# A planner that keeps its clocks from every instruction instead of from guesses

## The chip, the cores and the metric

The kernel runs on one core of one Trainium2 chip. The metric is the device time of one execution in microseconds (us). The core has five engines with instruction queues of their own: TensorE (PE in the profile; PEld is its weight load), VectorE (DVE), ScalarE (ACT), GpSimd (POOL) and SyncE (SP), which issues most of the DMAs here. Each engine works through its instructions in the order in which they were written; between engines, semaphores make an instruction wait for what it needs.

## The reference

One layer of a streaming encoder, on 2048 new frames of one stream (the prompt) and 64 frames of a running one (the sample), 1024 features:

```python
def mixer_layer(x, ln_g, w_in, lb, norm_g, w_out, attn_fn, s0):
    aq, ak, av, ag, hq, hf, hi, hg = jnp.split(rms_norm(x, ln_g) @ w_in, SPLITS, axis=-1)
    o_a = attn_fn(heads(aq), k, v).reshape(B, T, W_A) * jax.nn.silu(ag)
    o_b, S = hgrn2_branch(hq, hf, hi, hg, lb, norm_g, s0)
    y = x + jnp.concatenate([o_a, o_b], axis=-1) @ w_out
    return y, k, v, S
...
y_prompt = rms_norm(hp, ln_f_g)
```

The input projection is 1024 x 4096. Its columns feed two groups: group A, chunked attention (8 heads of 64; each chunk of 64 frames sees itself and the 8 chunks before it, plus a learned bias by relative distance, then a gate `silu(ag)`), and group B, a gated linear recurrence (HGRN2, 4 heads of 128, a norm per head, and a gate). The output projection is 1024 x 1024, then come the residual and a last RMSNorm. Outputs are the frames of prompt and sample, the newest K and V rows, and the states of the recurrence. All is float32.

## The kernel before, in words

**Precision.** TensorE takes a rounded float32 format here. To keep float32 accuracy, each factor is split into a high and a low part (`xh`, `xl` for the normalized and transposed x; `w[:, 0]`, `w[:, 1]` for a tile of weights), and a product is xh·w_hi + xl·w_hi + xh·w_lo. With 8 tiles along the 1024 features, one output tile is a group of 24 matmuls into one PSUM bank `acc` (`project`, recorded at L246, like nearly every matmul). There are two `acc` banks, and a group can only begin once the bank's former content has been read by ACT or DVE.

**Stages.** The frames are worked through in four super-blocks (512, 512 + 64 sample, 512, 512 frames). For each, `JOBS` lists 32 projection tiles of 128 columns, in the order hf, hq, hi, hg (group B), pg, pq, pk, pv (group A), for each of the four heads or pairs of heads. Blocks are 512 frames wide, 256 + 320 in the second super-block; the first two tiles and the last two of each super-block are worked in two halves, because the rows of the next x replace those of the old one half by half. In the first super-block the weights come raw from memory and are split by DVE and POOL (`w_split`, L461 to L469), then stored to be loaded in split form later.

**Beside the projections** run threads for:
- x (`x_tile`, `x_split`): load of 128 rows, square and sum (ACT L375), 1/root (ACT L343, L344), normalize (DVE L383), transposes on PE (L250) and the split into xh (ACT L408) and xl (DVE L412);
- the evacuations: silu of the gates (ACT L566 to L568), q (ACT L715, L721), k (ACT L738, L745, DVE L749), v (ACT L761);
- attention: score matmuls into the one `s` tile (two banks), softmax (DVE L819, L840, ACT L836), transposes of the probabilities, their split (ACT L848, DVE L851), the product with v (`pv`);
- the recurrence, with small matmuls of 32 rows (L254).

**The output phase.** W_out is applied by a seven-product scheme in the manner of Strassen, for eight pairs of 128-row tiles. A step (`out_step`) is 12 matmuls of 512 columns into one bank. Beside it, `out_parts` copies the next left factor's high part (ACT), `out_low` takes its low part (DVE L1597 or POOL L1589), sums of the factor's blocks are made (DVE L1610, POOL L1615), `out_adds` adds a bank to the kept partial `u` (DVE L1711) and to the residual rows (`out_add`, DVE L1685; the adds of `u` on POOL L1690), and `out_norm` makes the last norm (DVE L1753 or L1762). The residual rows and their room carry the names of former tiles (`xn`, `bias`, `pr`, `rest`). Part of W_out is loaded into the room of attention's v (L1930), once that is done.

**The order** is written by a planner, `Plan`, when the program is built. Every thread is a Python generator that yields what it waits for: a point in time, an engine, a buffer's token (`Tok`), or a condition. The main thread yields between pairs of matmuls; at each yield `pump` runs every thread that is ready, by priority, and what a thread writes goes to the end of its engine's queue. Readiness goes by the plan's estimated clocks: `C.now` for PE, `C.free` for ACT, DVE, POOL and SP. The threads themselves move these clocks: `C.act(n, t)`, `C.dve`, `C.pool` and `C.dma` add a time from flat formulas, with a width n that the thread gives, and `C.mm` adds a matmul. A thread that wants an engine is ready when that engine's clock is at most QUEUE (800 ns) ahead. The estimates set only the order; the waits on the chip come from the data.

Of the kernel before, what the change touches and what calls it, by code (L numbers as in the profile page):

```python
# [32 lines left out]
QUEUE = 800.0  # L33
# [12 lines left out]
JOBS = [[(k, g) for g in range(4) for k in ("hf", "hq", "hi", "hg", "pg", "pq", "pk", "pv")] for _ in SUPER]  # L46
JOBS[-1][-12:] = [("hf", 3), ("hq", 3), ("pq", 2), ("pk", 2), ("pv", 2), ("hi", 3), ("hg", 3), ("pg", 2), ("pg", 3),
# [3 lines left out]
class Plan:  # L51
# [4 lines left out]

    def __init__(self):
        self.now = 0.0
        self.free = {"A": 0.0, "D": 0.0, "P": 0.0, "S": 0.0}
        self.threads = []  # L60
        self.count = 0

# [65 lines left out]
    def mm(self, n, slow=False):  # L128
        self.now += 10.0 + 1.66 * n if slow else 12.0 + n / 2.37
# [12 lines left out]
    def dve(self, n, t=0.0):  # L142
        return self._on("D", 150.0 + 1.05 * n, t)

    def pool(self, n, t=0.0):
        return self._on("P", 300.0 + 1.6 * n, t)
# [34 lines left out]
def hymba_step(  # L181
# [24 lines left out]
    act = nc.scalar  # L206
    dve = nc.vector
    pool = nc.gpsimd
    pe = nc.tensor
    sp = nc.sync  # L210

    act.preload_act_table_set("natural_log_exp_and_others")
# [7 lines left out]
    C = Plan()  # L220
    uid = [0]

    def T(pool_, shape, dt, tag, **kw):
        uid[0] += 1
        return pool_.tile(list(shape), dt, tag=tag, name=f"{tag}_{uid[0]}", **kw)
# [19 lines left out]
    def mm(out, w, x, n, slow=False, **kw):  # L245
        pe.matmul(out, w, x, **kw)  # L246
        C.mm(n, slow)

    def transpose(out, x, idn):
        pe.transpose(out, x, idn)  # L250
        C.now += 110.0

    def mm32(out, w, x):
        pe.matmul(out, w, x, start=True, stop=True)  # L254
        C.now += 30.0
# [102 lines left out]
    def x_tile(sb, half, c, here=None, gain=None):  # L358
# [10 lines left out]
        if half and not sb:  # L369
            yield lambda: x_there.get((0, 0, 0), (0, 0))[0] == 4  # L370
        yield "A", t
        yield from tk["ck"].get()
        junk = T(wk, [P, D], mybir.dt.bfloat16, "ck", bufs=1)
        ss = T(wk, [P, 1], F32, "ss", bufs=4)
        act.activation(junk[:rows], xn[:rows], AF.Square, accum_out=ss[:rows])  # L375
        r = rstd_of(ss, rows, D)
        tk["ck"].put()
# [5 lines left out]
        dve.scalar_tensor_tensor(xn[:rows], xn[:rows], r[:rows], g, ALU.mult, ALU.mult)  # L383
        t = C.dve(1070, t)
# [49 lines left out]
    def weights():  # L434


        for j, (sb, nt) in enumerate(order):
            if sb:
# [5 lines left out]
                w_at[j] = (w, t, t)  # L444
# [10 lines left out]
    def w_split(j, nt, raw, t, tok):  # L455
# [12 lines left out]
        for k in range(0, KT, 2):  # L468
            pool.tensor_sub(w[:, 1, k : k + 2], raw[:, k : k + 2], f32(w[:, 0, k : k + 2]))  # L469
            t = C.pool(320, t)  # L470
            if k == 0:
                w_at[j] = (w, th, t + 2500.0)
            if k < KT - 2:
                yield "P", t - 300.0
        if tok:
            tk[tok].put()
# [4 lines left out]
    def out_weights():  # L481


        for a in range(4):
# [12 lines left out]
            def split(i, src):  # L497
# [3 lines left out]
                for c in cols:  # L501
                    yield "A", t
                    act.copy(f32r(st[:, c]), src[:, c])  # L503
                    t = C.act(256, t)
                    yield "P", t
                    pool.tensor_sub(f32r(st[:, c.start + 512 : c.stop + 512]), src[:, c], st[:, c])  # L506
                    t = C.pool(320, t)
                sp.dma_start(wod[i][:, :, a], st.rearrange("p (h c) -> p h c", h=2))
                state["t"] = t
                state[state["n"] - 1] = C.dma(512, t) + 2000.0  # L510

            def minus(out, x, y):
                for c in cols:
                    yield "P", state["t"]
                    pool.tensor_sub(out[:, c], x[:, c], y[:, c])
                    state["t"] = C.pool(320, state["t"])
# [10 lines left out]
            for tag, n in (("raw", 2), ("xn", 2), ("ck", 1)):  # L527
                tk[tag].put(n, C.now + 4000.0)
            yield C.now + 6000.0

    def project(j, ranges, evac, close=True, ready=None):
        yield lambda: j in w_at
        w, th, tl = w_at[j]
# [3 lines left out]
        for off, bn in ranges:  # L537
# [50 lines left out]
    def split_k(src, kd, c0, n, t):  # L588
        c = slice(c0, c0 + n)
        for h in range(2):  # L590
# [5 lines left out]
            if h == 0:  # L596
                yield "A", t - 300.0
# [14 lines left out]
    def load_bias(sb, p, d):  # L612
# [19 lines left out]
        C.now += 870.0  # L632
# [4 lines left out]
        tk["g"].put(1, t + 800.0)  # L637
# [45 lines left out]
    def pair_jobs(sb, p):  # L683
# [26 lines left out]
        def ev_q(acc, off, bn, t):  # L710
# [12 lines left out]
            yield "D", t - 600.0  # L723
            for h in range(2):
# [3 lines left out]
                if h == 0:  # L728
                    yield "D", t - 300.0
# [4 lines left out]
        def ev_k(acc, off, bn, t):  # L734
# [12 lines left out]
            yield "D", t - 600.0  # L747
# [1321 lines left out]
```

## Time and profile before

| | |
|---|---|
| median of three runs | 1264.97 us (1262.31 to 1268.16) |
| the profiled execution's own time | 1265.17 us |
| its span, first to last instruction | 1263.5 us |
| PE busy | 1243.6 us, 98% |
| DVE, ACT, POOL busy | 885.0, 698.6, 405.9 us |
| mean granted clock of TensorE | 0.995 |

The page gives the busy time of each engine, the chain of work that ended last, and groups of instructions. A wait of an engine is put down to what ended it: "PE acc L246 <- ACT vT L761" is a matmul into an acc bank that began when ACT's instruction of line 761 had ended. Busy time of PE counts a matmul also where the clock granted to TensorE is half; the granted clock of a stretch stands beside it. In a timeline a row gives its start, its duration, the engine, the line, out<-in, the shape and in brackets the idle time before it with its releaser.

### The profile page before, as it was taken

To read this page: it belongs to the slowest core of one execution; us is meant where nothing else is said; L and a number is where in the kernel's file an instruction comes from. 1 tells how busy PE (TensorE), PEld (TensorE's weight loads), DVE (VectorE), ACT (ScalarE), POOL (GpSimd) and SP (SyncE) were. 2 spreads that over 40 slices of the span, in tenths; PEclk is the share of its full clock that TensorE was granted. 3 is DMA by queue.
4 is the path that set the end of the run, shared out by engine and by line. 5 is a ranking of instruction groups with operands and counts; after the bars stand their busy time and mean duration, and the time that the engine had idled before them with its cause. 6 is when DMAs were issued, how large, how long until landed. Compare 5 with 4: busy or idle time off the path is not lost.

```text
span 1263.5 us, 22305 instructions
## 1 busy us (share of the span) xinstructions
PE 1243.6 (98%) x8182; PEld 1094.1 (87%) x8182; DVE 885.0 (70%) x1836; ACT 698.6 (55%) x1544; POOL 405.9 (32%) x704
## 2 busy tenths in 40 slices
PE   9999999999999999999999999999999999999997
PEld 8888888999999999998888888898888888878786
DVE  6787969676757667687575757685757765867775
ACT  5353646555655557575465556574646545643443
POOL 6655555111110111100242331133152203474543
PEclk9999999999999999999999999999999999999999
DMA  7876788635454455534858586557676476887331
GB/s 300 285 290 234 255 276 316 226 136 189 145 195 165 146 194 178 173 133 151 307 185 303 184 294 211 203 197 260 222 250 219 155 255 241 309 276 219 127 132 67
DMA packets 94862, 271.72 MB, mean 215 GB/s; under 512 B 10337, under 2 KB 43105, under 8 KB 77090
## 3 DMA queue, kind: packets, MB, share of 16 engines
q1 hardware_dynamic: 94464, 270.30, 60.7%
q8 instruction: 64, 1.05, 0.3%
q14 instruction: 44, 0.36, 0.1%
q10 hardware_dynamic: 290, 0.01, 0.0%
HBM read 186.66 MB, written 83.62 MB: 214 GB/s over the span
## 4 chain that ended last, share of the span: by engine, by line
PE 88%; DVE 4%; POOL 2%; ACT 2%; issue 2%; DMA 0%; SPq 0%; POOLq 0%; DVEq 0%; ACTq 0%
PE acc L246 62%; PE tr L250 6%; PE pv L246 6%; PE s L246 6%; PE g L246 5%; PE g L250 1%; PE g L254 1%; DVE slot L1597 1%; PE g L1864 1%; POOL sig L1615 1%; DVE xn L1685 1%; POOL xn L1690 1%; DVE xl L412 0%; POOL bias L1690 0%; DVE xn L1753 0%
## 5 line engine op out<-in xcount | busy, mean ns | idle before, releaser
L246 PE MATMUL acc<-xh,w 128*128 128x512 f32 (+2 forms) x2752 | 569.7, 346 | 5.9 <-ACT vT L761 2.1
L246 PEld LDWEIGHTS acc<-xh,w 128*128 128x128 f32 x2752 | 439.0, 190 | 56.5 <-ACT vT L761 2.3
L246 PE MATMUL acc<-xl,w 128*128 128x512 f32 (+2 forms) x1376 | 297.5, 348 | 0.2 <-DVE xl L412 0.2
L246 PEld LDWEIGHTS acc<-xl,w 128*128 128x128 f32 x1376 | 222.0, 190 | 25.8 <-issue 1.0
L819 DVE CUSTOM_DVE_ANT_0 pr<-s,bias 128x640 f32<-128x640 f32 (+4 forms) x128 | 94.3, 737 | 64.2 <-PE s L246 63.5
L848 ACT CAST ph<-tr 128x512 fp32r<-128x512 f32 (+3 forms) x176 | 88.1, 508 | 68.0 <-PE tr L250 36.4
L469 POOL TENSOR_TENSOR w<-wraw,w 128x256 fp32r<-128x256 f32 x120 | 98.9, 853 | 66.2 <-DVE w L464 41.1
L851 DVE TENSOR_TENSOR ph<-tr,ph 128x512 fp32r<-128x512 f32 (+3 forms) x176 | 100.5, 589 | 22.2 <-ACT ph L848 21.2
L836 ACT ACTIVATE pr<-pr,nm 128x640 f32<-128x640 f32 (+4 forms) x132 | 100.6, 762 | 25.2 <-DVE nm L819 24.6
L246 PE MATMUL pv<-ph,v 128*128 128x256 f32 (+2 forms) x344 | 97.7, 370 | 0.0
L250 PE MATMUL tr<-ident,pr 128*128 128x128 f32 x580 | 88.9, 272 | 1.1 <-DVE ph L851 1.1
L506 POOL TENSOR_TENSOR xn<-wraw,xn 128x256 fp32r<-128x256 f32 x48 | 37.8, 791 | 162.3 <-ACT xn L503 162.2
L988 POOL TENSOR_TENSOR mixa<-mixa,sga 128x256 f32<-128x256 f32 (+1 forms) x36 | 29.8, 826 | 171.9 <-DVE mixa L890 161.8
L890 DVE TENSOR_TENSOR mixa<-mixa,pv 64x256 f32<-64x256 f32 (+1 forms) x144 | 56.8, 395 | 35.0 <-ACT mixa L886 31.4
L250 PEld LDWEIGHTS tr<-ident,pr 128*128 128x128 f32 x580 | 70.5, 140 | 11.6 <-issue 1.5
L840 DVE TENSOR_SCALAR pr<-pr,sm 128x640 f32<-128x640 f32 (+4 forms) x132 | 76.9, 583 | 4.7
L1435 POOL TENSOR_TENSOR k<-ob 128x512 f32<-128x512 f32 (+2 forms) x20 | 17.8, 892 | 183.8 <-ACT ob L1426 183.8
L566 ACT ACTIVATE sig<-acc 128x512 f32<-128x512 f32 (+2 forms) x63 | 31.9, 506 | 60.7 <-PE acc L246 60.5
L246 PEld LDWEIGHTS pv<-ph,v 128*128 128x128 f32 (+1 forms) x344 | 58.1, 189 | 6.6
L246 PE MATMUL s<-kd,q 128*128 128x320 f32 (+3 forms) x232 | 56.4, 313 | 0.7 <-DVE nm L819 0.7
L246 PE MATMUL s<-kd,ql 128*128 128x320 f32 (+3 forms) x232 | 55.6, 310 | 0.0
L1458 POOL TENSOR_TENSOR ob<-ob,gg 128x512 f32<-128x512 f32 (+2 forms) x20 | 23.5, 1174 | 85.7 <-DVE ob L1454 66.5
(328 smaller groups left out, 2144.1 us busy)
## 6 DMA issues: line engine op xcount, KB each, us to landing
w<-wd SPq DMA_DIRECT2D x96, 1024.0 KB, 4.9
wd<-w SPq DMA_DIRECT2D x32, 1024.0 KB, 6.3
wraw<-in_w_in_dram SPq DMA_DIRECT2D x30, 512.0 KB, 4.9
wod<-xn SPq DMA_DIRECT2D x28, 512.0 KB, 3.6
xn<-in_x_prompt_dram SPq DMA_DIRECT2D x23, 512.0 KB, 6.0
bias<-biasd SPq DMA_DIRECT2D x12, 640.0 KB, 8.2
carry<-kd SPq DMA_DIRECT2D x12, 512.0 KB, 7.2
carry<-v SPq DMA_DIRECT2D x12, 512.0 KB, 5.8
```

Of the source, the lines that this page charges most:

```text
L246: pe.matmul(out, w, x, **kw)
L250: pe.transpose(out, x, idn)
L469: pool.tensor_sub(w[:, 1, k : k + 2], raw[:, k : k + 2], f32(w[:, 0, k : k + 2]))
L506: pool.tensor_sub(f32r(st[:, c.start + 512 : c.stop + 512]), src[:, c], st[:, c])
L566: act.activation(sig[:, :bn], acc, AF.Exp, scale=-1.0)
L819: dve.tensor_tensor_reduce(s[:, :nk].rearrange("p (a c) -> p a c", a=ns), sps[:, :ns, :kn], d.bias[:, h, bcol : bcol + nk].rearrange("p (a ...
L836: act.activation(s[:, :nk], s[:, :nk], AF.Exp, bias=nm[:, 0:1], scale=-1.0, accum_out=sm)
L840: dve.tensor_scalar(s[:, :nk], s[:, :nk], sm, None, ALU.mult)
L848: act.copy(ph[:krows, 0, :wid], pt[:krows, :wid])
L851: dve.tensor_sub(ph[:krows, 1, :wid], pt[:krows, :wid], f32(ph[:krows, 0, :wid]))
L890: dve.tensor_add(mix[hs, :qn], mix[hs, :qn], pv[hs, i, :qn])
L988: pool.tensor_mul(mix[:, :n], mix[:, :n], d.sg[:, g0 : g0 + n])
```

## The change: clocks charged per instruction, engines picked by them

Every engine is wrapped (`Queue`). Each instruction that is written charges the plan: a duration by engine, operation, width and whether an operand lies in PSUM; and its start is the latest of the engine's clock and of the last accesses to the same parts of the tiles it touches (`seen`, by boxes), with a lag for the engine that made the access. The functions `act`, `dve`, `pool` and `dma` now only answer when the engine's last instruction ends plus the lag; the widths in the threads are no longer read.

```diff
-QUEUE = 800.0
+QUEUE = 600.0
...
+JOBS[0][:2] = [("hq", 0), ("hf", 0)]
...
+    LAG = {"": 0.0, "T": 200.0, "A": 250.0, "D": 250.0, "P": 250.0, "S": 100.0}
...
+    def charge(self, e, ns, outs, ins):
+        t = max([self._last(e, x, True) for x in outs] + [self._last(e, x, False) for x in ins] + [0.0])
+        if e == "T":
+            self.now = end = max(self.now, t) + ns
+        elif e == "S":
+            start = max(self.now, self.free[e], t)
+            self.free[e] = start + 420.0
+            self.links = max(start + 520.0, self.links) + ns
+            self.landed = end = self.links + 2000.0
+        else:
+            self.free[e] = end = max(self.free[e], t) + ns
+        for x in ins:
+            self._note(e, x, False, end)
+        for x in outs:
+            self._note(e, x, True, end)
+        return end
+
+    def pick(self, t, **cost):
+        return min(cost, key=lambda e: max(self.free[e], self.now, t) + cost[e])
...
     def pe(self):
-        return self.now + 400.0
-
-    def _on(self, e, ns, t):
-        start = max(self.now, self.free[e], t)
-        self.free[e] = start + ns
-        return start + ns + 150.0
-
-    def act(self, n, t=0.0):
-        return self._on("A", 150.0 + 0.87 * n, t)
...
-    def dma(self, kbytes, t=0.0):
-        start = max(self.now, self.free["S"], t)
-        self.free["S"] = start + kbytes * 2.8
-        return self.free["S"] + 3500.0
+        return self.now + self.LAG["T"]
+
+    def act(self, n=0, t=0.0):
+        return self.free["A"] + self.LAG["A"]
...
+    def dma(self, kbytes=0, t=0.0):
+        return self.landed + self.LAG["S"]
...
+        if self.e == "S":
+            return _bytes(aps) / 370.0
```

(`_bytes` is four times the elements, more where the rows are short: 512 KB count 1417 ns.)

The output phase asks the clocks for the engine. Until the last super-block's attention is done, the answer is POOL:

```diff
+    def out_engine(t):
+        if done_a.get(len(SUPER) - 1, 0) < NPAIR * WIN:
+            return "P"
+        return C.pick(t, D=670.0, P=1500.0)
+
     def out_low(i, k, m, src, t, tags):
-        e = "P" if i < 2 and k != 3 else "D"
+        e = out_engine(t)
...
-                if op == ALU.add:
-                    yield "D", t
+                if out_engine(C.now) == "D":
+                    yield "D", C.now
                     dve.tensor_tensor(out, x, y, op)
...
-        if e == "D":
+        if e == "D" or out_engine(t) == "D":
             yield "D", t
             dve.tensor_add(x, x, part)
```

Other edits go with it. The threads' own allowances go: tokens are given back at an engine's time instead of `now + 800`, waits of `t - 300` or `t - 600` become `t - 100`; `project` waits until a weight tile's low part has been written out instead of 2.5 us after its high part:

```diff
-                w_at[j] = (w, th, t + 2500.0)
+                w_at[j] = [w, th, None]
...
+        w_at[j][2] = t
...
                 if i == 2:
-                    yield tl
+                    yield lambda: w_at[j][2] is not None
+                    yield w_at[j][2]
```

At the start, the first two tiles' normalize is written in two halves, the sum tile is made before the wait for `ck`, the gain row is loaded on SP's queue instead of ACT's, and the two first jobs change places:

```diff
-        dve.scalar_tensor_tensor(xn[:rows], xn[:rows], r[:rows], g, ALU.mult, ALU.mult)
-        t = C.dve(1070, t)
+        for cs in (slice(0, 512), slice(512, D)) if not sb and not half else (slice(0, D),):
+            dve.scalar_tensor_tensor(xn[:rows, cs], xn[:rows, cs], r[:rows], g[:, cs], ALU.mult, ALU.mult)
+        t = C.free["D"] - 600.0 * (not sb and not half)
...
-        act.dma_start(g_in[0:1], ln_in_g.rearrange("(o d) -> o d", o=1))
+        sp.dma_start(g_in[0:1], ln_in_g.rearrange("(o d) -> o d", o=1))
```

In `out_weights` the copies of a block are written before its subtractions, and the store waits for POOL's time. In the last super-block, whose x has no successor, the last two tiles are no longer worked in halves:

```diff
-                if u in (1, len(JOBS[sb]) - 1):
+                first, end = u < 2, not last and u >= len(JOBS[sb]) - 2
+                if (first or end) and u % 2:
...
-                elif u not in (0, len(JOBS[sb]) - 2):
+                elif not (first or end):
                     yield from project(j, blocks, evac)
```

More of the change, by code (lines that the diff above doesn't have):

```diff
@@ L148, in dma, with name, _box @@
-    def dma(self, kbytes, t=0.0):
-        start = max(self.now, self.free["S"], t)
-        self.free["S"] = start + kbytes * 2.8
-        return self.free["S"] + 3500.0
+    def name(self, pool, tag, bufs, name):
+        n = self.rooms.setdefault((pool, tag), [0])
+        n[0] += 1
+        self.rooms[name] = (pool, tag, n[0] % bufs)
+    def _box(self, ap):
+        name = getattr(ap.tensor, "source_name", None)
+        room = self.rooms.get(name)
+        if room is None or room[1] in ("xh", "xl"):
+            return None, None
+        dims = [tuple(d) for d in ap.ap]
+        if room[0] == "dr":
+            return room, (0, 1, ap.offset, ap.offset + 1 + sum((n - 1) * st for st, n in dims))
+        p, f = divmod(ap.offset, dims[0][0])
+        return room, (p, p + dims[0][1], f, f + 1 + sum((n - 1) * st for st, n in dims[1:]))
@@ new lines, in _last, with _note @@
+    def _last(self, e, ap, write):
+        room, box = self._box(ap)
+        t = 0.0
+        for b, (w, r) in self.seen.get(room, {}).items():
+            if b[0] < box[1] and box[0] < b[1] and b[2] < box[3] and box[2] < b[3]:
+                for at, by in (w, r) if write else (w,):
+                    if by != e:
+                        t = max(t, at + self.LAG[by])
+        return t
+    def _note(self, e, ap, write, end):
+        room, box = self._box(ap)
+        if room is None:
+            return
+        boxes = self.seen.setdefault(room, {})
+        w, r = boxes.get(box, ((0.0, ""), (0.0, "")))
+        boxes[box] = ((end, e), r) if write else (w, max(r, (end, e)))
@@ new lines, in pick, with dve, pool, _free @@
+    def pick(self, t, **cost):
+        return min(cost, key=lambda e: max(self.free[e], self.now, t) + cost[e])
+    def pe(self):
+        return self.now + self.LAG["T"]
+    def act(self, n=0, t=0.0):
+        return self.free["A"] + self.LAG["A"]
+    def dve(self, n=0, t=0.0):
+        return self.free["D"] + self.LAG["D"]
+    def pool(self, n=0, t=0.0):
+        return self.free["P"] + self.LAG["P"]
+    def dma(self, kbytes=0, t=0.0):
+        return self.landed + self.LAG["S"]
+def _free(ap):
+    n = 1
+    for d in list(ap.ap)[1:]:
+        n *= d[1]
+    return n
@@ L154, with _bytes, _size @@
+def _bytes(aps):
+    n = min(_size(x) for x in aps)
+    run = min(list(x.ap)[-1][1] if list(x.ap)[-1][0] == 1 else 1 for x in aps)
+    return 4.0 * n * max(1.0, 128.0 / run)
+def _size(ap):
+    n = 1
+    for d in list(ap.ap):
+        n *= d[1]
+    return n
 class Tok:
@@ L767, in ev_v @@
             d.v_t = max(d.v_t, C.now + 1000.0)
-            if last and p == NPAIR - 1 and d.v_n == n:
-                have.add("projected")
+            closing()
             if d.v_n == n and not last:
@@ L799, in ev_g, with closing @@
             d.sg_n += bn
+            closing()
+        def closing():
+            if last and p == NPAIR - 1 and d.v_n == n and d.sg_n == n:
+                have.add("projected")
         return d, dict(g=ev_g, q=ev_q, k=ev_k, v=ev_v)
@@ L1140, in ev_f @@
             act.activation(f[:, :bn], acc, AF.Exp, scale=-1.0)
-            tk["acc"].put(1, C.now + 800.0)
+            tk["acc"].put(1, C.act())
             act.activation(f[:, :bn], f[:, :bn], AF.Ln, bias=one_t)
@@ L1448, in rec_block @@
         act.activation(rs[:, :bn], pn[:, :bn], AF.Ln, bias=eps_t, scale=1.0 / P)
-        tk["g"].put(1, C.now + 800.0)
+        tk["g"].put(1, C.act())
         act.activation(rs[:, :bn], rs[:, :bn], AF.Exp, scale=-0.5)
@@ L1921, in program @@
                 j += 1
+            if last:
+                x_left[sb, 0] = x_left[sb, 1] = True
         for i, k in steps:
```

157 lines of the change are left out of this document (109 added, 48 removed).

## The prediction

> **What bounds the kernel now.** I read the page's busy shares and its chain first, then the chain of waits of TensorE, then stage windows, then the timelines around each gap.
>
> ```profile
> span 1263.5 us, 22305 instructions
> PE 1243.6 (98%) x8182; PEld 1094.1 (87%) x8182; DVE 885.0 (70%) x1836; ACT 698.6 (55%) x1544; POOL 405.9 (32%) x704
> PE 88%; DVE 4%; POOL 2%; ACT 2%; issue 2%; DMA 0%; SPq 0%; POOLq 0%; DVEq 0%; ACTq 0%
> ```
>
> PE is busy 1243.6 of 1263.5 us. The change leaves the arithmetic alone, so it can only win from the 19.9 us in which PE idles, and from stretches in which PE runs at a lower clock. Two parts of the idle time are out of reach: the start and the tail. The columns of a stage window are us, PE, PEld, DVE, ACT, POOL busy, clock, DMA share, GB/s.
>
> ```profile
> 0.00:13.50 13.50, 11.74 (x58) 10.06 (x59) 4.40 (x6) 6.22 (x13) 6.63 (x21) 0.87 0.87 324
> 254.30:257.70 3.40, 3.40 (x16) 3.40 (x15) 3.33 (x13) 2.13 (x8) 0.66 (x3) 0.50 0.02 5
> 810.60:814.00 3.40, 3.40 (x16) 3.40 (x17) 2.34 (x5) 2.97 (x8) 0.00 (x0) 0.51 1.04 433
> 1066.60:1070.00 3.40, 3.06 (x25) 3.07 (x26) 2.49 (x6) 1.09 (x4) 0.00 (x0) 1.00 1.01 367
> 1128.00:1131.40 3.40, 3.40 (x16) 2.79 (x15) 3.40 (x3) 1.14 (x2) 3.40 (x3) 1.00 1.16 316
> 1137.60:1256.90 119.30, 118.25 (x517) 95.55 (x515) 84.44 (x128) 48.79 (x121) 57.45 (x66) 1.00 0.42 135
> 1256.90:1263.50 6.60, 0.01 (x1) 0.00 (x0) 3.43 (x5) 1.22 (x4) 0.00 (x0) 0.83 0.42 159
> ```
>
> The tail costs 6.59 us and the start 1.76; 11.5 us of idle remain. Two stretches of 3.4 us, one behind each of the two largest gaps of the middle, ran at a granted clock of 0.50 and 0.51: each loses 3.4 x 0.5 = 1.7 us of work. So the most the change can win is about 11.5 + 3.4 = 14.9 us and a little of the program's own length. The waits name the gaps:
>
> ```profile
> PE acc L246 <- ACT vT L761: 2.1, 1, 2.1
> PE acc L246 <- ACT xh L408: 1.7, 2, 1.3
> PE acc L246 <- DMA v<-wod: 1.7, 1, 1.7
> PE acc L246 <- ACT vT L738: 1.4, 1, 1.4
> PE tr L250 <- DVE ph L851: 1.1, 1, 1.1
> PE s L246 <- DVE nm L819: 0.7, 1, 0.7
> PE acc L246 <- DVE pr L1685: 0.6, 1, 0.6
> PE acc L246 <- DVE xn L1685: 0.6, 2, 0.4
> ```
>
> Each is a single event, a place where the written order put a matmul a little too early. Nothing is spread over the run.
>
> **The change part by part.** *Clocks from instructions, waits per tile (Plan.charge, QUEUE 600, LAG).* No instruction changes by this; the order does. I compared the two written orders at each gap.
>
> ```profile
> 253.89 0.61 PE L246 MATMUL acc<-xh,w 128*128 128x320 f32 x2 [1.34 <-ACT xh L408]
> 810.56 1.16 PE L246 MATMUL acc<-xh,w 128*128 128x256 f32 x4 [2.08 <-ACT vT L761]
> 810.13 0.37 ACT L761 COPY vT<-acc 128x256 f32<-128x256 f32 x1 [0.69 <-DVE kd L749]
> 1062.44 1.21 PE L246 MATMUL acc<-xh,w 128*128 128x256 f32 x8 [0.45 <-ACT vT L715]
> 1066.94 0.98 PE L246 MATMUL acc<-xh,w 128*128 128x256 f32 x6 [1.37 <-ACT vT L738]
> 1066.53 0.35 ACT L738 COPY vT<-acc 128x256 f32<-128x256 f32 x1
> 1126.96 0.50 PE L246 MATMUL acc<-v,slot 128*128 128x512 f32 x1 [1.66 <-DMA v<-wod]
> ```
>
> At 253.9 the first 320-wide matmul stands right behind the last transposes of the next x rows, so PE waits while ACT and DVE turn them into xh and xl. In the new order 12 matmuls of 256 columns stand between; by the pitch (1.21 - 0.98) / 2 = 0.115 us each that is 1.4 us, as long as the gap. Gain 1.34, and the slow stretch behind it. At 810.6 the acc bank was emptied late because its copy (L761) was queued on ACT behind k work that itself waited 0.69 us for DVE; the new order leaves at least 1.6 us of PE work between a bank's last matmul and its next first one there. Gain 2.08, and its slow stretch. The two stretches are worth 1.7 each at most and nothing at least, if another gap starts one; I take 1.5 each, because gaps as long remain at few places. At 561 the 0.7 us wait for the softmax has at least 1.3 us of work before it: gain 0.67. At 1106 the transpose's wait for a split (1.1) has more too: gain 1.1. At 1062 to 1067 two gaps, 0.45 + 1.37, stand against one place of the new order where a 512-wide acc group of pk follows directly on the evacuation of pq: an evacuation of a 256-wide bank takes 0.35 us, and one of 512 with its wake-up I put at 0.95 us (between 0.45 and 1.37, the gaps of such a place). Gain 0.87.
>
> At 1127 PE waits for W_out rows loaded into v's room, which comes free only with the last pv. The loads' queue does not change; but 58 matmuls stand between the last pv and the first use where there were 28, and at 118.25 / 517 = 0.229 us each that is 30 x 0.229 = 6.9 us more. Gain 1.66; at worst, if the loads queue behind others by 5 us more, still all of it.
>
> *Last super-block unsplit.* 96 matmuls of 256 columns become 48 of 512.
>
> ```profile
> 1135.69 5.70 PE L246 MATMUL acc<-w,slot 128*128 128x512 f32 x24 [0.25 <-DVE bias L1685]
> 1240.28 3.00 PE L246 MATMUL acc<-w,slot 128*128 128x512 f32 x12 [0.41 <-DVE xn L1685]
> 7.05 3.75 PE L1864 MATMUL g<-ident 128*128 128x128 f32 x22
> ```
>
> A 512-wide matmul costs (5.70 - 3.00) / 12 = 0.225, two of 256 cost 0.230: 48 x 0.005 = 0.2 us gained.
>
> *The start.* Swapped hf and hq cost nothing, since both tiles' weights are loaded before either is done. The gain row's load moves onto SP's queue ahead of the x loads and delays them by one small issue; ends 0 and +0.5, and I take 0, because PE spins until the first transposes anyway. One spin less (10 for 11, 3.75 / 11) is 0.3 gained, if the first half-width normalize is done by then.
>
> *The output phase.* In before, the sums for the Strassen products, the low parts and the adds of u are fixed to POOL or DVE; now each goes to the engine free first. By the orders 56 POOL instructions of 256 columns go away there, and about 28 DVE ones of 512 come.
>
> ```profile
> 1239.45 0.69 DVE L1685 TENSOR_TENSOR xn<-xn,acc 128x512 f32<-128x512 f32 x1 [1.27 <-POOL xn L1690]
> 1238.68 0.73 POOL L1690 TENSOR_TENSOR xn<-xn,asb 128x256 f32<-128x256 f32 x1
> 1236.98 1.74 POOL L1615 TENSOR_TENSOR sig<-sig,reset 128x256 f32<-128x256 f32 x1
> L1685 DVE TENSOR_TENSOR xn<-xn,acc 128x512 f32<-128x512 f32 x14 | 9.4, 684 | 9.0 <-PE acc L246 4.4 <-POOL xn L1690 3.2 <-ACT asb L1703 1.3
> L1597 DVE TENSOR_TENSOR slot<-sig,slot 128x512 fp32r<-128x512 f32 x11 | 8.1, 748 | 0.0
> L1610 DVE TENSOR_TENSOR vT<-vT,vT 128x512 f32<-128x512 f32 x3 | 3.1, 1036 | 0.2 <-POOL sig L1615 0.2
> L1753 DVE SCALAR_TENSOR_TENSOR xn<-xn,rstd,gin 128x1024 f32<-128x1024 f32 (+1 forms) x6 | 8.1, 1355 | 3.1 <-ACT rstd L1748 3.1
> 1127.13 3.43 DVE L1753 SCALAR_TENSOR_TENSOR xn<-xn,rstd,gin 128x1024 f32<-128x1024 f32 x2
> ```
>
> The gap of 0.41 at 1240 is DVE's add waiting 1.27 us, in order, behind POOL's u-add, itself behind a POOL sum of 1.74 us: with the u-adds on DVE this chain is gone. Of the waits on L1685 (0.6 + 0.6 + 0.3) I count 1.2 gained. What it costs: 28 x 0.684 = 19 us more on DVE, which is busy 84.4 of 119.3 us; 103 of 119 (87%) stays under the matmuls as long as no step of 12 matmuls (2.7 us) waits for its bank. I take 1 us lost there; ends 0 and 18 (the rival below). The Trainium skill, "Perfetto Trace Analysis", section "Optimizing Scalar/DVE Operations", says that a saturated DVE should give work away, and that moving work between DVE and GpSimd may not help, since they share an SBUF port. This case's trace agrees in part: the normalize took 3.43 / 2 = 1.72 us beside a POOL sum, against a mean of 1.355. By that rule the move would give nothing in this phase, and the sum would be 1.2 us worse.
>
> *What the tighter order costs.* The new lags (0.2 to 0.25 us) leave less room than the old guesses. Two kinds of places:
>
> ```profile
> L819 DVE CUSTOM_DVE_ANT_0 pr<-s,bias 128x640 f32<-128x640 f32 (+4 forms) x128 | 94.3, 737 | 64.2 <-PE s L246 63.5
> xn<-in_x_prompt_dram SPq DMA_DIRECT2D x23, 512.0 KB, 6.0
> 810.53 1.06 ACT L375 ACTIVATE ck<-xn 128x1024 bf16<-128x1024 f32 x1
> 247.00 0.29 ACT L343 ACTIVATE rstd<-ss,eps 128x1 f32<-128x1 f32 x1
> ```
>
> About ten groups of score matmuls now have 1.20 to 1.36 us of PE work since the scores bank was filled before, which must cover 0.737 for the softmax row and a wake-up on both sides. I put 0.15 us on each: 1.5, ends 0 and 3. And at the first boundary of super-blocks an x row tile is loaded 9.0 us of PE work before its transposes (14.3 before). The path needs 6.0 to land, 1.06 for the square, 0.29 for each of the root's two small steps and 1.355 for the normalize: 9.0. I take 0.5 us, ends 0 and 1.5 plus a slow stretch of 1.7.
>
> **Sum.** Gained: 1.34 + 2.08 + 2 x 1.5 + 0.67 + 1.1 + 0.87 + 1.66 + 0.2 + 0.3 + 1.2 = 12.4. Lost: 1.0 + 1.5 + 0.5 = 3.0. Net 9.4: span 1254.1. The profiled execution took 1265.17 us with a span of 1263.5, so 1.7 lies around it, and it stands 0.2 above the median of 1264.97. So 1255.6.
>
> **The rivals.** *Eaten by tight lags.* The gaps go, but the micro-waits come at their upper ends (3 for scores, 3.2 for x rows) and new gaps of a microsecond arise where the per-tile clocks are wrong, each starting a slow stretch as at 254 and 810. For it: a gap of 1.34 was enough for that, and PE has no slack elsewhere. Against it: behind the gaps of 1.37 at 1066 and 1.66 at 1126 the windows show a clock of 1.00. With 4 to 5 us more it ends near 1260 to 1264, within 0.5%.
>
> The Trainium skill, "TensorE: Matmul & The Clock Gate", Part 1, ties the slowdown to an idle window of about 3.4 us; here the trace shows gaps of 1.34 and 2.08 us in front of it, so the length of a gap alone does not tell.
>
> *DVE becomes the bound of the output phase (slower).* Per pair of row tiles there are seven steps, 84 x 0.229 = 19.2 us of PE. All elementwise work on DVE would be 7 x 0.748 + 11 x 0.684 + 4 x 1.036 + 2 x 1.355 = 19.6 us. The picker prices DVE at 0.67 and POOL at 1.5, so it leans that way. It decides when DVE's 103 us, grown by collisions as the normalize was (1.72 / 1.355 = 1.27), pass 119: 131, 12 us over, and with in-order waits of 0.15 us on some 44 steps another 6. Then 1255.6 + 12 + 6 - 1 = about 1272. For it: a step would then need 19.6 / 7 = 2.80 us of DVE and has 2.74 of PE. Against it: with less on POOL there are fewer collisions.
>
> *The clocks do not hold.* The planner assumes that a 512 KB load lands about 3.9 us after its issue (520 + 512 KB / 370 + 2000, in ns), where 6.0 is measured; then the order is as blind as before at loads and the other gains halve: 1259 to 1261.
>
> **How the numbers follow.** About what a measurement can tell from no change is 0.5%, 6.3 us. My forecast, gaps gone at small cost: 0.60, 1250 to 1258.5. Eaten or not holding: 0.22, of which 0.03 below the threshold's 1258.6 and 0.19 within. DVE bound: 0.18, two thirds of it (0.15) slower than 1271.3, the rest within or under. So faster 0.63, same 0.22, slower 0.15. The low end is all gaps gone at no cost, 1263.5 - 14.9 - 0.5 + 1.7 - 0.2 = 1249.6. The high end takes in the eaten case and part of the DVE one: 1268.
>
> **What would show it.** Right: no wait of PE on the evacuations of v and q at the boundaries, none on the load of W_out into v's room, clock 1.00 there, PE idle near 11 us, DVE 85 to 88% busy in the last 120 us. Wrong: a wait of PE on DVE's adds or low parts in many output steps; waits on x rows at 230 to 245 us; a row of waits on the softmax of more than 3 us; PE busy itself longer, by slow stretches at new places.

## The result and the profile after

The changed kernel takes 1280.74 us (median of four runs, 1279.89 to 1283.07), the kernel before 1264.26 beside it. The ratio is 1.0129, 95% interval 1.0101 to 1.0157: slower by some 16 us, where 9 us faster was forecast. The profiled execution of the changed kernel took 1283.07 us.

All engines now go through one wrapper, so every instruction of the changed kernel carries the line L227 and is told by its tiles. First the page of the changed kernel (span, busy time, the chain that ended last):

```profile
span 1281.4 us, 22104 instructions
PE 1249.2 (97%) x8132; PEld 1089.1 (85%) x8132; DVE 891.6 (70%) x1861; ACT 699.7 (55%) x1539; POOL 361.1 (28%) x648
PE 69%; DVE 5%; issue 2%; ACT 2%; DMA 2%; POOL 1%; SPq 0%; DVEq 0%; ACTq 0%; POOLq 0%
```

PE idles 32.2 us of the span where it idled 19.9. To see where, I cut both spans at the same places of the program: the first projection matmul, the first 320-wide one (the end of super-block 0), the last matmul. The windows of the kernel before, then those of the changed one (us, PE, PEld, DVE, ACT, POOL busy, clock, DMA share, GB/s; the changed kernel's second part stands in two rows):

```profile
13.50:253.90 240.40, 237.65 (x1525) 201.67 (x1525) 188.94 (x357) 128.77 (x272) 129.97 (x197) 1.00 0.75 269
253.90:1256.60 1002.70, 993.94 (x6600) 882.42 (x6600) 688.27 (x1470) 562.40 (x1257) 269.31 (x486) 1.00 0.58 201
```

```profile
15.40:274.40 259.00, 245.58 (x1542) 204.87 (x1543) 194.34 (x383) 132.78 (x282) 138.58 (x194) 0.99 0.70 250
274.40:1130.60 856.20, 849.12 (x5919) 759.06 (x5918) 571.90 (x1288) 498.70 (x1091) 195.41 (x410) 1.00 0.60 209
1130.60:1274.40 143.80, 140.53 (x619) 114.57 (x617) 117.71 (x182) 60.94 (x150) 21.21 (x25) 1.00 0.51 160
```

Super-block 0 takes 259.0 us instead of 240.4 (17 matmuls of 8100 have moved into it); all that follows takes 1000.0 instead of 1002.7. The start is 1.9 us longer, the tail 0.1. So the loss lies in super-block 0, where the kernel before had hardly a wait, and the gain forecast for the rest did not come. The four largest waits of TensorE in super-block 0 of the changed kernel (us in total, times, longest):

```profile
PE g L227 <- DVE k L227: 6.0, 5, 2.5
PE pv L227 <- DVE ph L227: 2.1, 3, 0.7
PE s L227 <- DVE nm L227: 1.7, 1, 1.7
PE g L227 <- DVE asb L227: 1.3, 3, 0.6
```

The kernel before waited 1.6 us in all there, ahead of the 1.34 us at 253.9 that close the stage. The first row is the recurrence: its small 32-row matmuls wait for `k`, made by DVE. The timeline of the changed kernel around one of them, PE, DVE and POOL:

```profile
106.59 1.01 PE L227 MATMUL g<-q,k 128*32 128x64 f32 x52 [0.99 <-DVE k L227]
105.25 0.43 DVE L227 TENSOR_TENSOR q<-q,fq 128x256 f32<-128x256 f32 x1 [1.50 <-POOL fq L227]
105.59 0.94 DVE L227 TENSOR_TENSOR k<-k,fk 128x256 f32<-128x256 f32 x1
100.76 1.24 POOL L227 TENSOR_TENSOR mixa<-mixa,sga 128x256 f32<-128x256 f32 x1 [2.79 <-DVE mixa L227]
101.94 0.66 POOL L227 MEMSET pf<- 128x16 f32 x1
105.29 2.98 POOL L227 TENSOR_TENSOR w<-wraw,w 128x256 fp32r<-128x256 f32 x3
```

PE waits for DVE, which waited 1.50 us for POOL, which was late. POOL had itself stood 2.79 us waiting for DVE's `mixa`; then a multiplication of 256 columns that the plan charges at 745 ns (330 + 1.62 x 256) took 1.24 us, with DVE at work beside it; and the four memsets and nine copies and products of a few columns that follow took 3.4 us (101.94 to 105.34), where the plan charges 2.1 (40 + n for a memset, 200 + 2.2 n for the others). DVE's `k` then took 0.94 us beside POOL's subtractions for the weights (the last row); the same shape in the row above it took 0.43. For instructions of 256 and 512 columns the plan's durations are those of instructions that run alone.

### The profile page after: what moved, and what is told of

Its sections match the earlier page's. It is cut to its first block, busy times and chain, and to the rows that moved or that the text cites. A ratio compares the mean times of both kernels' runs of the same rounds, so it can differ in the third digit from the quotient of the medians.

```text
span 1281.4 us, 22104 instructions
## 1 busy us (share of the span) xinstructions
PE 1249.2 (97%) x8132; PEld 1089.1 (85%) x8132; DVE 891.6 (70%) x1861; ACT 699.7 (55%) x1539; POOL 361.1 (28%) x648
## 4 chain that ended last, share of the span: by engine, by line
PE 69%; DVE 5%; issue 2%; ACT 2%; DMA 2%; POOL 1%; SPq 0%; DVEq 0%; ACTq 0%; POOLq 0%
PE acc L227 50%; PE g L227 6%; PE tr L227 5%; PE s L227 5%; PE pv L227 4%; DVE xn L227 1%; DVE pr L227 1%; DMA xn<-in_x_prompt_dram 1%; DMA wraw<-mixd 1%; ACT sig L227 0%; ACT ck L227 0%; POOL xn L227 0%; DVE mixa L227 0%; DMA w<-wd 0%; DVE asb L227 0%
## 5 line engine op out<-in xcount | busy, mean ns | idle before, releaser
L227 PE MATMUL acc<-xh,w 128*128 128x512 f32 (+2 forms) x2720 | 572.9, 349 | 1.1 <-ACT vT L227 0.7
L227 PEld LDWEIGHTS acc<-xh,w 128*128 128x128 f32 x2720 | 435.5, 189 | 51.5 <-issue 2.5
L227 PE MATMUL acc<-xl,w 128*128 128x512 f32 (+2 forms) x1360 | 293.5, 348 | 0.3 <-DVE xl L227 0.3
L227 PEld LDWEIGHTS acc<-xl,w 128*128 128x128 f32 x1360 | 220.8, 189 | 26.7 <-DVE xl L227 0.5
L227 POOL TENSOR_TENSOR mixa<-mixa,sga 128x256 f32<-128x256 f32 (+1 forms) x36 | 30.7, 853 | 354.1 <-DVE mixa L227 282.5
L227 ACT ACTIVATE pr<-pr,nm 128x640 f32<-128x640 f32 (+4 forms) x132 | 100.7, 763 | 50.6 <-DVE nm L227 50.0
L227 DVE CUSTOM_DVE_ANT_0 pr<-s,bias 128x640 f32<-128x640 f32 (+5 forms) x144 | 100.9, 705 | 38.6 <-PE s L227 38.1
L227 ACT CAST ph<-tr 128x512 fp32r<-128x512 f32 (+3 forms) x176 | 87.9, 508 | 69.1 <-PE tr L227 36.9
L227 POOL TENSOR_TENSOR w<-wraw,w 128x256 fp32r<-128x256 f32 x120 | 105.8, 910 | 62.9 <-DVE w L227 48.3
L227 DVE TENSOR_TENSOR ph<-tr,ph 128x512 fp32r<-128x512 f32 (+3 forms) x176 | 101.4, 590 | 13.5 <-ACT ph L227 12.3
L227 PE MATMUL pv<-ph,v 128*128 128x256 f32 (+2 forms) x344 | 97.5, 370 | 3.2 <-DVE ph L227 2.1
L227 PE MATMUL tr<-ident,pr 128*128 128x128 f32 x580 | 91.0, 274 | 3.0 <-DVE ph L227 1.7
L227 PEld LDWEIGHTS tr<-ident,pr 128*128 128x128 f32 x580 | 70.0, 140 | 15.1 <-issue 1.9
L227 ACT ACTIVATE sig<-acc 128x256 f32<-128x256 f32 (+2 forms) x86 | 42.6, 496 | 66.7 <-PE acc L227 62.0
L227 DVE TENSOR_SCALAR pr<-pr,sm 128x640 f32<-128x640 f32 (+4 forms) x132 | 73.5, 557 | 4.7
L227 DVE TENSOR_TENSOR mixa<-mixa,pv 64x256 f32<-64x256 f32 (+1 forms) x144 | 56.8, 394 | 20.9 <-ACT mixa L227 17.7
L227 PEld LDWEIGHTS pv<-ph,v 128*128 128x128 f32 (+1 forms) x344 | 58.0, 189 | 14.0 <-DVE ph L227 3.7
L227 ACT ACTIVATE sig<-sig 128x512 f32<-128x512 f32 (+2 forms) x109 | 57.5, 528 | 10.6 <-DVE gk L227 7.7
L227 ACT COPY vT<-acc 128x512 f32<-128x512 f32 (+2 forms) x64 | 31.1, 486 | 50.2 <-PE acc L227 50.1
L227 POOL TENSOR_TENSOR k<-ob 128x512 f32<-128x512 f32 (+2 forms) x20 | 18.2, 911 | 143.0 <-ACT ob L227 138.9
L227 PE MATMUL s<-kd,q 128*128 128x320 f32 (+3 forms) x232 | 56.7, 314 | 1.8 <-DVE nm L227 1.7
L227 POOL TENSOR_TENSOR xn<-wraw,xn 128x256 fp32r<-128x256 f32 x48 | 38.7, 821 | 65.4 <-ACT xn L227 65.4
```

The lines of the kernel that those rows point to most:

```text
L227: r = f(*args, **kw)
```

## The experiments

The theory from this profile: **collisions**. DVE and POOL lengthen each other's instructions where both read SBUF, the new durations leave no room for that, and super-block 0 is where POOL is busy (139 of 259 us, with the weights' low parts; 22% behind it). The rivals: too small **margins** as such, **loads** that land later than planned (5.7 us for a raw weight tile against 3.9), and the edits of the **start**. All times below stand beside runs of the kernel before on the same chip, 1265.6 to 1266.5 us. Gains in microseconds are told against the changed kernel's 1280.74; by the ratios to the kernel before, which was 1 to 2 us faster beside that run than beside these, some are up to 3 us larger.

**The plan's DVE and POOL stretched in super-block 0.**

```diff
     def charge(self, e, ns, outs, ins):
+        if self.first and e in "DP":
+            ns *= 1.25
```

> The changed kernel, with the durations that the plan charges to DVE and POOL made 1.25 times as long while super-block 0 is written; nothing else. If the loss in super-block 0 comes from durations measured without collisions (DVE's 512-wide two-operand instructions planned at 0.668 us took 0.905 there, POOL's 256-wide ones planned at 0.745 took 0.920), the waits of the recurrence's small matmuls for DVE go (6.5 us) with most of the others there, and the time falls by 8 to 14 us, to 1267 to 1273. If the loads' landing time or the start is the cause, it stays within 3 us of 1280.7.

Measured 1265.69 us, ratio to before 1.0013 (0.9997 to 1.0030): 15 us gained, the whole loss, where 8 to 14 were expected. Its windows, cut at the same places:

```profile
12.30:253.20 240.90, 237.91 (x1524) 201.93 (x1525) 192.53 (x356) 127.78 (x269) 133.71 (x197) 1.00 0.75 270
253.20:1255.00 1001.80, 993.01 (x6554) 875.75 (x6552) 699.72 (x1495) 563.16 (x1254) 216.90 (x430) 1.00 0.58 201
```

Super-block 0 is back at 240.9. The plan is mended by charging longer durations in that stage alone; the collisions are still there (`k<-k,gk` takes a mean of 0.882 us in this run's super-block 0, `bl<-k,sf` 1.090). Stretching one engine at a time tells which:

> The changed kernel with the durations charged to POOL alone 1.25 times as long in super-block 0. If it is POOL's weight splits that are planned too short (0.745 us against 0.920) and so the recurrence's small factors and the adds behind them that come late, this alone gives most of what stretching both gave (15 us): 1265 to 1270. If DVE's are what matters: 1276 to 1281.

> The changed kernel with the durations charged to DVE alone 1.25 times as long in super-block 0. If DVE's planned times are the cause (0.668 us against 0.905 for the 512-wide ones with two inputs in SBUF), 1265 to 1270; if POOL's are: 1276 to 1281. If both are needed, each of the two gives 4 to 9 us.

POOL alone 1273.54 (1.0050, 1.0032 to 1.0067), DVE alone 1269.19 (1.0020, 1.0007 to 1.0034): 7 and 12 us, 10 and 14 by the ratios. Neither is enough by itself, DVE's is worth more: with it alone super-block 0 takes 243.1 us (16.1 to 259.2), with POOL's 251.0 (15.6 to 266.6).

**The same order without the collisions.** This run changes the chip's work, not the order. POOL writes zeros instead of subtracting; the weights' low parts in super-block 0 are left out of the result.

```diff
-            pool.tensor_sub(w[:, 1, k : k + 2], raw[:, k : k + 2], f32(w[:, 0, k : k + 2]))
+            for _ in range(3):
+                nc.gpsimd.memset(f32(w[:, 1, k : k + 2]), 0.0)
+            C.charge("P", 745.0, [w[:, 1, k : k + 2]], [raw[:, k : k + 2], w[:, 0, k : k + 2]])
```

> The changed kernel, every engine's order as it is there, but POOL writes zeros into the weights' low parts in super-block 0 (three memsets of 256 columns, some 0.8 us together, for each subtraction that took 0.743 undisturbed) instead of subtracting; the weights' low parts are left out of the result, and the plan charges the subtraction all the same. If collisions of POOL's reading instructions with DVE's are the cause, DVE's 512-wide instructions in super-block 0 fall from a mean of 0.905 to 0.75 or less, the waits of the recurrence for DVE from 7.5 to under 3 us, and the time by 8 us or more, to 1272 or less. If the plan is wrong for another reason (loads, wake-ups), waits and time stay within 3 us of 1280.7.

Measured 1270.32 us, 1.0033 (1.0021 to 1.0044): 10 us gained, 12 by the ratios. Groups of instructions in super-block 0 (busy us, mean ns), first of the changed kernel, then of this run:

```profile
L227 DVE TENSOR_TENSOR k<-k,gk 128x512 f32<-128x512 f32 x8 | 6.2, 779 | 0.1
L227 DVE TENSOR_TENSOR bl<-k,sf 128x512 f32<-128x512 f32 x4 | 4.9, 1216 | 0.0
L227 POOL TENSOR_TENSOR w<-wraw,w 128x256 fp32r<-128x256 f32 x117 | 103.7, 915 | 62.8 <-DVE w L227 48.3 <-issue 13.7 <-POOL w L227 0.8
```

```profile
L227 DVE TENSOR_TENSOR k<-k,gk 128x512 f32<-128x512 f32 x8 | 5.5, 683 | 0.1
L227 DVE TENSOR_TENSOR bl<-k,sf 128x512 f32<-128x512 f32 x4 | 2.7, 684 | 0.0
L620 POOL MEMSET w<- 128x256 f32 x365 | 126.8, 363 | 32.1 <-PE acc L227 18.1
```

POOL is busy for longer with the weights than in the changed kernel (126.8 us against 103.7), but it no longer reads, and DVE's instructions fall to one and the same time: 1216 ns to 684, 779 to 683. The largest waits of PE in this run's super-block 0, and the window:

```profile
PE g L227 <- DVE bias L227: 1.3, 2, 0.7
PE acc L227 <- DVE xn L227: 0.8, 1, 0.8
PE g L227 <- DVE k L227: 0.7, 2, 0.4
```

```profile
15.70:261.40 245.70, 241.44 (x1542) 204.07 (x1543) 177.38 (x381) 132.60 (x282) 154.15 (x434) 1.00 0.73 261
```

The recurrence's waits for `k` fell from 6.0 to 0.7 us, super-block 0 from 259.0 to 245.7 with the same 1542 matmuls.

The memsets change one thing more: they need not wait for DVE's copies of the weights, for which POOL stood idle 48.3 us in the changed kernel. That is not where the gain comes from in the recurrence. At the place of the timeline above, DVE still waits 1.21 us for POOL (1.50 there), and it is its own `k` that is shorter, 0.42 us for 0.94:

```profile
100.56 1.01 PE L227 MATMUL g<-q,k 128*32 128x64 f32 x52 [0.35 <-DVE k L227]
99.75 0.43 DVE L227 TENSOR_TENSOR q<-q,fq 128x256 f32<-128x256 f32 x1 [1.21 <-POOL fq L227]
100.09 0.42 DVE L227 TENSOR_TENSOR k<-k,fk 128x256 f32<-128x256 f32 x1
```

PE's wait fell from 0.99 to 0.35 us. The Trainium skill, "SBUF — State Buffer", section "SBUF: two separate sides", says that a DVE instruction with two inputs in SBUF and a GpSimd instruction that reads SBUF exclude each other for a whole instruction. The trace agrees on what collides: 1216 ns against 684, and POOL's memsets, which read nothing, cost these instructions nothing. That the exclusion lasts a whole instruction is not shown by it.

**The control: the same on the kernel before.**

> The control: the kernel before, its order as it is, with the same three memsets in place of each subtraction of the weights' low parts in super-block 0 (those low parts are left out of the result). If the collisions cost time only where the order leaves no room for them, this kernel, whose waits in super-block 0 came to 1.6 us, gains less than 2 us: 1264 to 1267 beside 1266.0 of before on that chip. If the memsets shorten super-block 0 by themselves, whatever the order, it gains as much as the changed kernel did, some 10 us: 1256.

Measured 1266.28 us, 1.0010 (0.9995 to 1.0025): no gain. The collisions are there too in the kernel before (its `k<-k,fk`, 256 wide, took 0.956 us in the same stage), but its order has room for them. So the collisions are no cause by themselves; they cost time under an order that was written without them. Of the 16 us, 10 to 12 are shown to be theirs. The rest is not assigned; Some of POOL's small instructions are planned too short in any stage (`pf<-eb` of 4 columns is charged 0.21 us and took a mean of 0.46 in super-block 0, 0.43 between 560 and 1000 us); that was not tested by itself.

**Flat durations.** The per-tile accesses stay; ACT, DVE and POOL are charged by the old formulas of the width alone.

```diff
+        if name != "dma_start" and self.e in "ADP":
+            return {"A": 150.0 + 0.87 * n, "D": 150.0 + 1.05 * n, "P": 300.0 + 1.6 * n}[self.e]
```

> The changed kernel, with tile accesses and per-engine charges as they are, but ACT, DVE and POOL charged by the former flat formulas of the instruction's width (150 + 0.87 n, 150 + 1.05 n, 300 + 1.6 n ns), without regard to operation and memory. If the finer durations are too short where engines collide, the longer flat ones for DVE (0.688 instead of 0.668 for 512 in SBUF, 0.688 instead of 0.620 in PSUM, 0.822 instead of 0.724 for a 512-wide half of a copy) give little: 1274 to 1281. If coarse durations were as good as fine ones all along and the tile accesses do the harm, it stays at 1280 within 3; if the fine ones do it: below 1270.

Measured 1268.89 us, 1.0019 (1.0006 to 1.0031). The coarser durations are 12 us better than the finer ones, and my bound for "little" was wrong: it went by small differences (688 ns for 668), and for one input the flat formula charges far more, 688 ns instead of 407 for `gk`, 512 wide, and 1225 instead of 724 for the copy of a raw weight tile, 1024 wide. `gk` of the changed kernel in super-block 0, then in a quiet stage (560 to 1000 us):

```profile
L227 DVE TENSOR_SCALAR gk<-sig 128x512 f32<-128x512 f32 x3 | 2.5, 848 | 0.1
L227 DVE TENSOR_SCALAR gk<-sig 128x512 f32<-128x512 f32 x5 | 2.1, 428 | 0.2
```

In the quiet stage it takes 428 ns, as the fine formula has it (407); in super-block 0 848. So for `gk` the flat formula was nearer to what super-block 0 needs, for the wrong reason; for the copies, which took 781 ns there, it was simply longer. Which of the longer charges gained the time, this run does not tell: ACT's and POOL's changed with them.

**Margins.**

```diff
-QUEUE = 600.0
+QUEUE = 850.0
-    LAG = {"": 0.0, "T": 200.0, "A": 250.0, "D": 250.0, "P": 250.0, "S": 100.0}
+    LAG = {"": 0.0, "T": 200.0, "A": 500.0, "D": 500.0, "P": 500.0, "S": 100.0}
```

> The changed kernel with the lags of ACT, DVE and POOL 500 ns instead of 250 and QUEUE 850 instead of 600, in all super-blocks. If it is margin as such that is missing, as little as a quarter of a microsecond per hand-over, the time falls by 8 us or more, to 1272 or less, and waits of 0.2 to 0.4 us go everywhere. If collisions in super-block 0 are the cause, waits there of 0.9 to 2.5 us shrink by a quarter of a microsecond each only: 1276 to 1279. If loads or the start are the cause: 1280 within 3 us.

Measured 1263.48 us, 0.9977 (0.9964 to 0.9991). More than the collision theory allowed: my bound of a quarter of a microsecond per wait was wrong, because a chain PE - DVE - POOL - DVE has several hand-overs, and each gets the margin. In super-block 0 it mends half (250 us for 259), and the rest of its gain lies behind it.

**Loads.** The plan's landing time 3800 ns instead of 2000.

> The changed kernel with the plan's landing time of a load 1.8 us longer (2000 to 3800 ns, so that 512 KB land 5.7 us after the issue, as measured). If instructions that wait in order for loads (DVE's copy of a raw weight tile, the bias's loads) hold up the queues in super-block 0, the time falls by 6 us or more, to 1274 or less. If collisions are the cause, it stays within 3 us of 1280.7.

Measured 1271.29 us, 1.0041 (1.0027 to 1.0056). By its own expectation this spoke for the loads. The next pair tells it otherwise.

**All three, and without the loads.** Both have the stretch in super-block 0 and the wider margins; the first has the longer landing time too.

> The changed kernel with DVE and POOL charged 1.25 times in super-block 0, lags of 500 ns and QUEUE 850, and the landing time longer by 1.8 us, all three. Each alone gave 15, 17 and 9 us. If they mend different places (collisions in super-block 0; small gaps behind it; loads), super-block 0 goes to before's 240 us with the short gaps of super-blocks 2 and 3: 1254 to 1260, faster than both kernels by 4 us or more. If they all mend the same place, it stays with the best of them: 1262 to 1266.

> As the run before it without the longer landing time. If loads are a cause of their own, this is 2 to 4 us slower than with it; if landing time only made room for collisions by the way, it is within 1.5 us of it: 1254 to 1260 as well.

With the loads 1263.04 us (0.9978, 0.9965 to 0.9991), without them 1260.16 (0.9969, 0.9954 to 0.9984). A longer landing time adds nothing once the other two are there, so the loads are no cause of their own that these runs could show; that a later landing, alone, gained 9 us because it moved work later by the way is argued, not shown. Both missed the 1254 to 1260 that they were given; with the loads the time lies where it was expected if all three mend the same place (1262 to 1266). The run without them has the lowest median of this study, 0.3% below the kernel before and 20 us below the changed one; its interval overlaps with that of the margins alone. Its windows:

```profile
16.40:257.80 241.40, 237.98 (x1528) 202.45 (x1528) 187.92 (x358) 129.32 (x272) 130.11 (x197) 1.00 0.74 264
257.80:1254.60 996.80, 991.33 (x6550) 877.28 (x6549) 693.82 (x1490) 561.77 (x1252) 224.70 (x434) 1.00 0.59 202
```

Against the run that is stretched alone, super-block 0 is the same (241.4 and 240.9), and what follows takes 996.8 instead of 1001.8: the margins are worth 5.0 us there. The listed waits of PE behind super-block 0 add up to 8.4 us in that run and to 5.3 in this one.

**The start.** Gain row back on ACT's queue, hf before hq, the normalize in one piece.

> The changed kernel with its edits of the start undone: the gain row loaded on ACT's queue, hf before hq, the normalize of the first tiles in one piece. If these edits make the start 2 us longer (first projection matmul at 15.4 instead of 13.5 us) and hold the clock low, the time falls by 2 to 3 us; if the late clock of the profiled execution was the chance of a free-running window, it stays within 1 us. Neither says that it comes below 1276.

Measured 1281.99 us, 1.0135 (1.0110 to 1.0159): no gain, and the first projection matmul came at 15.8 us. The edits of the start are not what made it long. The rows that differ are the four half-passes of the gain matmul, in the kernel before and in the changed one:

```profile
5.15 1.98 PE L1875 MATMUL s<-gin,asb 1*128 1x512 f32 x4
```

```profile
5.14 3.78 PE L227 MATMUL s<-gin,asb 1*128 1x512 f32 x4
```

The same four matmuls, begun at the same time, took nearly twice as long. Slower matmuls would point to the clock, but the profile grants 1.00 in both of these stretches, so it doesn't show a cause. The start with the plan stretched had 2.15 us there, the run below with the output phase's engines fixed 2.15 too, and its first projection matmul came at 11.85 us. What decides between the two stays open.

**The output phase's engines fixed as before.**

```diff
-        e = out_engine(t)
+        e = "P" if i < 2 and k != 3 else "D"
...
-                if out_engine(C.now) == "D":
+                if op == ALU.add:
...
-        if e == "D" or out_engine(t) == "D":
+        if e == "D":
```

> The changed kernel with the output phase's engines fixed as before (sums and adds of u on POOL, low parts of the first pairs too). If the pick by clocks is worth what the prediction gave it (1.2 us of waits gone, 1 us lost), nothing moves: 1279 to 1283. If DVE's added 19 us cost time, it falls to 1275 or less; if the collisions of POOL's 256-wide instructions with DVE's were worth more than the waits seen, it rises by 3 us or more.

Measured 1283.19 us, 1.0152 (1.0123 to 1.0181). Compared with the changed kernel's 1.0129, the pick gains rather than loses, about 2 us if anything; the two intervals overlap. Waits of PE from 1137 us on, in the changed kernel and in this run:

```profile
PE acc L227 <- DVE xn L227: 2.2, 1, 2.2
PE acc L227 <- ACT ck L227: 1.1, 1, 1.1
```

```profile
PE acc L227 <- DVE xn L227: 2.5, 4, 0.9
PE acc L227 <- DMA v<-wod: 1.7, 1, 1.7
PE acc L227 <- DVE pr L227: 0.7, 1, 0.7
PE acc L227 <- DVE bias L227: 0.6, 2, 0.4
```

With the fixed engines the adds' small waits and the wait for the load into v's room come back.

## Why the prediction was wrong

**The step that failed** is "What the tighter order costs", sized at 3.0 us in all with the output phase, and the sentence ahead of it that the clocks change no instruction, only the order, and that the orders were compared "at each gap". I looked where the kernel before waited. Super-block 0 had no gap to speak of, so I did not ask what the new order would do there. It lost 15 to 16 us (18.6 us longer, less some 3 for the 17 matmuls more). That the clocks change the order alone is true of the instructions written; their durations change with the order, 0.42 to 0.94 us for the `k` that PE waits for. Taking POOL's reads away under the same order gave 10 to 12 us back. The evidence was in my own rows: a normalize of 1.72 us against 1.355, which I used for the output phase alone. The stage to price collisions in was the one where POOL is busiest beside DVE.

**The gaps, one by one.** The waits of PE behind super-block 0, in the kernel before and in the changed one, show the rest:

```profile
PE acc L246 <- ACT vT L761: 2.1, 1, 2.1
PE acc L246 <- DMA v<-wod: 1.7, 1, 1.7
PE acc L246 <- ACT vT L738: 1.4, 1, 1.4
PE acc L246 <- ACT xh L408: 1.3, 1, 1.3
PE tr L250 <- DVE ph L851: 1.1, 1, 1.1
```

```profile
PE acc L227 <- DVE xn L227: 2.2, 1, 2.2
PE tr L227 <- DVE ph L227: 1.7, 3, 1.2
PE g L227 <- DVE k L227: 1.5, 2, 0.8
PE acc L227 <- ACT ck L227: 1.1, 1, 1.1
PE tr L227 <- DVE xl L227: 0.9, 2, 0.6
PE pv L227 <- DVE mixa L227: 0.8, 1, 0.8
PE acc L227 <- ACT vT L227: 0.7, 1, 0.7
```

- The gaps on the x rows (253.9) and on the evacuations (810.6, 1062 to 1067) are gone but for the one I had left standing (0.7 us on `vT`, put at 0.95); so are the softmax wait and the wait for the load into v's room. These steps were right.
- The wait of the transposes at 1106 (1.1) did not go: it stands at 1120 with 1.15 us.
- In place of the others came waits of about the same sum on the recurrence's `k`, the transposes, the attention's `pv` and, in the output phase, 2.2 us on DVE's adds. The listed waits behind super-block 0 add up to 10.3 us before and to 10.1 after. The rival "eaten by tight lags" had this, but I looked for it at the score matmuls, where no wait is listed behind super-block 0, and at the x rows of the first boundary, where 0.3 us came. That wider margins (lags and QUEUE together) win 5.0 us back there, with super-block 0 unchanged, shows that tight margins are what ate it.
- The slow stretches behind 254 and 810 are gone; a new one of 3.4 us stands behind the 2.5 us gap of super-block 0, as the rival said of new gaps:

```profile
45.78 1.01 PE L227 MATMUL g<-q,k 128*32 128x64 f32 x52 [2.52 <-DVE k L227]
47.10:50.50 3.40, 3.40 (x11) 2.62 (x10) 2.83 (x5) 0.00 (x0) 1.08 (x2) 0.50 0.95 282
```

- The slower rival, DVE as the bound of the output phase, did not happen: DVE was busy 117.7 of 143.8 us there (82%; 84% in the last 119.3 of them, where 85 to 88 was forecast), two waits of PE stand in it, and the fixed engines gave no gain. The kernel did get slower, but from another place: DVE and POOL colliding was a part of this rival's mechanism, and the stage was wrong.
- "The clocks do not hold" was a rival with loads as its reason; the clocks did not hold for instructions that collide.

What stays open is what makes the gain matmuls of the start take 2 us in some executions and 3.8 in others, and what the 4 to 6 us of the loss are that the run without POOL's reads did not give back.

## What to carry to other kernels

A planner with precise durations of single instructions writes a tight order, and a tight order is only as good as what it leaves out: here DVE and POOL reading SBUF together. Where the precise numbers come from instructions that ran alone, keep a margin, above all in the stage in which two engines lengthen each other's instructions; 25% on two engines in one stage and a quarter of a microsecond per hand-over made a loss of 16 us a gain of 4. And when an order is rewritten, price the stages without waits too: here that was where nearly all was lost.

## What was not expected of the hardware

- A DVE instruction of 512 columns with two inputs in SBUF took a mean of 1.216 us beside POOL's subtractions and 0.684 beside POOL's memsets, although POOL was busy for longer with the latter. For these it is not POOL's being busy that counts, but its reading.
- A DVE instruction with one input, `gk` of 512 columns, was lengthened as well: 0.428 us in a quiet stage, 0.848 in super-block 0, 0.496 there beside the memsets. The copies of raw weights, one input too, were not relieved by the memsets: 0.868 us beside them, 0.781 beside the subtractions.
- A single gap of 2.52 us of TensorE was followed by 3.4 us at a clock of 0.50, as gaps of 1.34 and 2.08 were in the kernel before; after a gap of 2.19 us that ended at 1151 in the changed kernel the clock stayed at 1.00.
